# Row-scale products of the output projection moved from GpSimd to VectorE, row copies to ScalarE

## The chip, the cores and the metric

One core of a Trainium2 chip runs the whole layer. The metric is device microseconds (us) of one execution; less is better. A core has five engines that run side by side, each through its own list of instructions in order: PE (TensorE, matrix products), DVE (VectorE), ACT (ScalarE), POOL (GpSimd) and SP (SyncE, which here only starts transfers). They wait for each other through semaphores. Matrix results land in PSUM, everything else is held in SBUF, and weights come from HBM by DMA.

## The reference

The layer has an attention part (two head groups), an output projection with a residual, a norm with a router, and a mixture of 32 experts; then a final norm. The change lies where the output projection meets the second norm:

```python
mix = jnp.concatenate([o_a, o_b.astype(x.dtype)], axis=-1) @ w_out[l]     # 256 x 2048 @ 2048 x 2048
x = x + g1 * mix
h2 = rmsnorm(x, norm2_g[l]) * (1.0 + sc2) + sh2                             # sh2, sc2, g1: rows of 2048
x = x + g2 * hierarchical_moe(h2, w_router_group[l], b_router_group[l], w_router_expert[l], ...)
...
def rmsnorm(x, g):
    r = lax.rsqrt(jnp.mean(x32 * x32, axis=-1, keepdims=True) + EPS)
    return (x32 * r).astype(x.dtype) * g
```

The router takes h2 @ w_router (36 columns), picks one of 4 groups and 2 of 8 experts for each of the 256 tokens. Every expert's weights (w1, w3: 2048 x 512, w2: 512 x 2048, float32) are read once.

## The kernel before, in words

**Up to the output projection** (about 590 us) the kernel computes the modulation rows, the input projection and the head groups. The rows g1, norm2_g * (1 + sc2) and others lie in the tile `MOD`, each as four pieces of 512 on partitions 0, 32, 64, 96.

**The output projection** goes through four column blocks n = 0..3 of 512 columns. For each, `proj` adds up the products of all 2048 rows in two PSUM tiles `acc[t]` (t: the two halves of 128 tokens). A float32 product is made of three faster ones: the weight piece `wr` (two rows of tiles, 512 KB, L366) is rounded by ACT to `wH` (L376), DVE takes the remainder `wL` (L382), and PE multiplies wH with both parts of the left side and wL with one. One piece is 12 matmuls on PE (8 with wH, 4 with wL, L421; L407 in the last pieces of block 3), here called a step. `wr` has five buffers, wH and wL three each, so the conversions run up to three steps ahead of PE, and SP loads a new `wr` once DVE is done with an old one.

**Behind each block** `mix_out(n, ...)` is fed in pieces between the matmuls of the next block:
- POOL spreads a piece of `MOD` over all 128 partitions, `g1b` for g1 and `G2b` for the norm's row (L1010, two buffers each).
- For each t: DVE multiplies acc with g1b to `tmp` (L1021) and adds it to the residual `X` (L1022); ACT squares and sums a row (L1023, into `sp`); the row is multiplied by G2b to `xg` (the row-scale product: L1027 on POOL for n < 3, L1030 on DVE for n = 3); and `xg` is copied in another order of columns to `h2p`, the experts' input (the row copy: L1028 on ACT for n < 3, L1031 on POOL for n = 3).
- PE transposes xg to `ptr` in two pieces k2 (L1039), ACT copies each to `xt` (L1044; DVE does the very last one, L1042), and PE multiplies it with the router's weights, `pre` (L1049).

Beside block 1 stand two small products of the router's constant row, `pc` (L1062, L1065, con L1067).

**After block 3** the sums in `sp` become the norm's factor (`rsq`: L184, L185, a power, on POOL), DVE picks the experts in a chain of some 50 small instructions, and PE starts on the experts: `gather` (L1248), up (L1272), down (L1366). The experts' weights come through eight SBUF tiles of 2 MB, `r2t` (four; loads start during the projection) and `r3t` (four; in space that the projection's tiles leave), and three tiles `r4t` of 1 MB.

**Order.** The front and the experts are written out by hand on PE and SP. In the stretch of the output projection a scheduler orders every engine's list by its own estimates when the kernel is built, so a moved instruction also moves others. On POOL, the broadcast and the ordinary arithmetic belong to two pieces of code: the builder puts an instruction `ISA` without operands ahead of the first of the other kind.

Of the kernel before, what the change touches and what calls it, by code (L numbers as in the profile page):

```python
# [7 lines left out]
F32 = mybir.dt.float32  # L8
# [3 lines left out]
AF = mybir.ActivationFunctionType  # L12
OP = mybir.AluOpType
# [3 lines left out]
P = 128  # L17
# [93 lines left out]
def block_kernel(ctx: ExitStack, tc: tile.TileContext, x, w_mod, w_gate, w_in, w_ab, w_out, w_router, w1, w3, w2, w2_last,  # L111
                 vecs, rows, small, consts, out, dbg=None):
    nc = tc.nc
# [325 lines left out]
    def proj(form, lh=None, ll=None, before=None, end=False):  # L439
        acc = acc_pair(ps_acc, "acc")  # L440
        for q in range(4):
            step(acc, form, lh or hHb, ll or hLb, 0, NJ - 1, before, end and q == 3)
            ada_n()
        if form == "T":
            return acc
        drain_urgent()
        return acc
# [548 lines left out]
    wp = lst.enter_context(tc.tile_pool(name="wp", bufs=1, side="right", reuse_waits="tile"))  # L996
# [12 lines left out]
    def bcast(dst, src, n):  # L1009
        nc.gpsimd.partition_broadcast(dst, src[32 * n:32 * n + 1])  # L1010
        return dst

    sp = wp.tile([P, 2, 4], F32, name="sp")
    pre = ps_w.tile([P, 2, 36], F32, name="pre", tag="pre")

    def mix_out(n, acc, g1b, G2b):
        xg = [wq.tile([P, 512], F32, name="xg", tag="xg", bufs=2) for _ in range(2)]
        for t in range(2):
            xs = X2[:, t, n * 512:(n + 1) * 512]
            tmp = wq.tile([P, 512], F32, name="tmp", tag="tmp", bufs=2)  # L1020
            nc.vector.tensor_tensor(tmp, acc[t], g1b, op=OP.mult)  # L1021
            nc.vector.tensor_tensor(xs, xs, tmp, op=OP.add)  # L1022
            nc.scalar.activation(tmp, xs, AF.Square, accum_out=sp[:, t, n:n + 1])  # L1023
            hd = h2p[:, t, :, 32 * n:32 * n + 32].rearrange("p j q -> p q j")
            xv = xg[t].rearrange("p (q j) -> p q j", j=NJ)
            if n < 3:
                nc.gpsimd.tensor_tensor(xg[t], xs, G2b, op=OP.mult)  # L1027
                nc.scalar.activation(hd, xv, AF.Copy)  # L1028
            else:
                nc.vector.tensor_tensor(xg[t], xs, G2b, op=OP.mult)  # L1030
                nc.gpsimd.tensor_copy(hd, xv)  # L1031
        for _ in range(OY):
            yield 1
        for k2 in range(2):
            pt = ps_w.tile([P, 2, T], F32, name="ptr", tag="w", bufs=2)
            for t in range(2):
                for a in range(2):
                    k = 2 * k2 + a
                    nc.tensor.transpose(pt[:, a, t * P:(t + 1) * P], xg[t][:, k * P:(k + 1) * P], ident)  # L1039
            xt = wq.tile([P, 2, T], F32, name="xt", tag="xt", bufs=2)  # L1040
            if n == 3 and k2:
                nc.vector.tensor_copy(xt, pt)  # L1042
            else:
                nc.scalar.activation(xt, pt, AF.Copy)  # L1044
            yield 1
            for a in range(2):
                m = 4 * n + 2 * k2 + a
                for t in range(2):
                    nc.tensor.matmul(pre[:, t], xt[:, a, t * P:(t + 1) * P], WR[:, m], start=m == 0 and t == 0,  # L1049
                                     stop=m == NJ - 1, skip_group_check=True)  # L1050
            yield 1

    for n in range(4):
        g1b = bcast(wq.tile([P, 512], F32, name="g1b", tag="g1b", bufs=2), MOD[:, 0], n)
        G2b = bcast(wq.tile([P, 512], F32, name="G2b", tag="G2b", bufs=2), MOD[:, 1], n)
        if n:
            acc = proj("B", mixH, mixL, end=n == 3)
        urgent.append(mix_out(n, acc, g1b, G2b))
        if n == 1:
            pc = ps_w.tile([P, 2, 64], F32, name="pc", tag="w", bufs=2)  # L1060
            for j in range(NJ):
                nc.tensor.matmul(pc[0:1, 0, 0:36], S2[:, j:j + 1], WP[:, j], start=j == 0, stop=j == NJ - 1)  # L1062
            cr = wp.tile([1, 36], F32, name="cr")
            nc.scalar.activation(cr, pc[0:1, 0, 0:36], AF.Copy)
            nc.tensor.matmul(pc[:, 1, 0:36], ones[0:1], cr, start=True, stop=True)  # L1065
            con = wp.tile([P, 36], F32, name="con")
            nc.vector.tensor_tensor(con, pc[:, 1, 0:36], SM[:, S_RG:S_RG + 36], op=OP.add)  # L1067
# [339 lines left out]
    for t in range(2):  # L1407
        for n in range(4):
            xs = X2[:, t, n * 512:(n + 1) * 512]
# [63 lines left out]
```

## Time and profile before

| what | us |
|---|---|
| three timed runs | 1648.83, 1653.0, 1654.01 (median 1653.0) |
| profiled execution, its own time | 1649.8 |
| its span, from the first to the last instruction of the program | 1648.1 |
| PE busy | 1509.4 (92%) |
| DVE busy | 695.3 (42%) |
| ACT busy | 369.3 (22%) |
| POOL busy | 115.5 (7%) |
| HBM read | 584.73 MB, 356 GB/s over the span |

A start time in a row counts from the first instruction of the program. Busy time says how long an engine was at work, not whether anybody waited for it; PE busy counts matmuls that overlap and runs of half clock alike. What the engines waited for stands in brackets behind a row of the timeline: [idle time before it <- who ended it]. "issue" there means that no other engine is seen to have held it. PEclk is the granted share of PE's full clock of 2.4 GHz: 1.00 is that, 0.50 is 1.2 GHz.

### The profile page before, as it was taken

To read this page: it belongs to the slowest core of one execution; us is meant where nothing else is said; L and a number is where in the kernel's file an instruction comes from. 1 tells how busy PE (TensorE), PEld (TensorE's weight loads), DVE (VectorE), ACT (ScalarE), POOL (GpSimd) and SP (SyncE) were. 2 spreads that over 40 slices of the span, in tenths; PEclk is the share of its full clock that TensorE was granted. 3 is DMA by queue.
4 is the path that set the end of the run, shared out by engine and by line. 5 is a ranking of instruction groups with operands and counts; after the bars stand their busy time and mean duration, and the time that the engine had idled before them with its cause. 6 is when DMAs were issued, how large, how long until landed. Compare 5 with 4: busy or idle time off the path is not lost. (4 is left out here: it accounts for less than half of the span.)

```text
span 1648.1 us, 20660 instructions
## 1 busy us (share of the span) xinstructions
PE 1509.4 (92%) x8517; PEld 892.8 (54%) x8517; DVE 695.3 (42%) x1085; ACT 369.3 (22%) x745; POOL 115.5 (7%) x139
## 2 busy tenths in 40 slices
PE   3999989799789979799999999999999999899996
PEld 1788857688678867644443444444344344244432
DVE  4677797777555653513222313322231231232223
ACT  3444453363333544200100000010000000000002
POOL 1000033232111011100000000000000000000002
PEclk9999999899899998899999999999999999899998
DMA  9989688587677565579999999999999999999995
GB/s 353 371 335 369 250 325 318 209 328 286 262 302 271 204 232 212 237 301 376 415 427 429 426 428 427 429 426 428 428 427 427 427 428 427 427 426 427 426 420 217
DMA packets 74359, 588.50 MB, mean 357 GB/s; under 512 B 14084, under 2 KB 14468, under 8 KB 36372
## 3 DMA queue, kind: packets, MB, share of 16 engines
q1 hardware_dynamic: 68596, 581.88, 86.7%
q10 hardware_dynamic: 5664, 5.24, 1.0%
q8 instruction: 69, 1.13, 0.3%
q14 instruction: 30, 0.25, 0.0%
HBM read 584.73 MB, written 2.10 MB: 356 GB/s over the span
## 5 line engine op out<-in xcount | busy, mean ns | idle before, releaser
L1272 PE MATMUL h<-r2t,heT 128*64 128x512 f32 x1024 | 333.6, 600 | 9.9 <-issue 6.2
L1272 PE MATMUL h<-r3t,heT 128*64 128x512 f32 x1024 | 330.4, 594 | 1.1 <-DMA r3t<-in_w_dram 1.1
L382 DVE TENSOR_TENSOR wL<-wr,wH 128x1024 fp32r<-128x1024 f32 x144 | 178.2, 1242 | 110.1 <-ACT wH L376 84.5
L1272 PEld LDWEIGHTS h<-r2t,heT 128*64 128x64 f32 x1024 | 105.1, 138 | 157.3 <-issue 150.9
L376 ACT ACTIVATE wH<-wr 128x1024 fp32r<-128x1024 f32 x144 | 151.9, 1057 | 150.1 <-PE acc L421 70.7
L1272 PEld LDWEIGHTS h<-r3t,heT 128*64 128x64 f32 x1024 | 104.4, 137 | 147.0 <-issue 143.6
L1366 PE MATMUL po<-r2t,hidT 128*64 128x512 f32 x488 | 157.7, 594 | 3.7 <-ACT hidT L1289 3.7
L1366 PE MATMUL po<-r3t,hidT 128*64 128x512 f32 x448 | 147.2, 594 | 3.7 <-ACT hidT L1289 3.7
L1248 PEld LDWEIGHTS pgt<-ohr,h2p 128*128 128x128 f32 x1024 | 117.4, 194 | 16.6 <-issue 16.6
L1248 PE MATMUL pgt<-ohr,h2p 128*128 128x128 f32 x1024 | 121.0, 280 | 2.0 <-DVE ohr L1229 2.0
L1304 DVE TENSOR_TENSOR po<-po,g2b 128x512 f32<-128x512 f32 x64 | 44.5, 695 | 182.7 <-PE po L1366 171.8
L1313 DVE TENSOR_TENSOR X<-X,py 128x512 f32<-128x512 f32 x128 | 82.2, 684 | 85.3 <-PE py L1311 85.3
L417 PE MATMUL acc<-hH,wH 128*128 128x256 f32 x640 | 101.1, 299 | 8.4 <-ACT wH L376 8.4
L417 PE MATMUL acc<-hH,wL 128*128 128x256 f32 x640 | 97.4, 293 | 9.9 <-DVE wL L382 9.9
L1280 DVE SCALAR_TENSOR_TENSOR eth<-eth,h 128x512 f32<-128x512 f32 x16 | 11.0, 688 | 221.4 <-ACT eth L1279 221.4
L1279 ACT ACTIVATE eth<-h 128x512 f32<-128x512 f32 x16 | 9.6, 597 | 407.5 <-PE h L1272 407.5
L417 PEld LDWEIGHTS acc<-hH,wH 128*128 128x128 f32 x640 | 86.5, 198 | 24.6 <-ACT wH L376 12.5
L417 PE MATMUL acc<-hL,wH 128*128 128x256 f32 x640 | 97.0, 293 | 0.0
L417 PEld LDWEIGHTS acc<-hH,wL 128*128 128x128 f32 x640 | 85.3, 195 | 20.2 <-DVE wL L382 12.1
L417 PEld LDWEIGHTS acc<-hL,wH 128*128 128x128 f32 x640 | 86.1, 197 | 5.5 <-issue 5.0
L1366 PEld LDWEIGHTS po<-r2t,hidT 128*64 128x64 f32 x488 | 49.1, 137 | 69.9 <-issue 64.5
L1305 ACT ACTIVATE ob<-po 128x512 fp32r<-128x512 f32 x64 | 38.2, 597 | 213.2 <-DVE po L1304 213.2
(354 smaller groups left out, 1724.8 us busy)
## 6 DMA issues: line engine op xcount, KB each, us to landing
r2t<-in_w_dram SPq DMA_DIRECT2D x90, 2048.0 KB
r3t<-in_w_dram SPq DMA_DIRECT2D x88, 2048.0 KB
at<-in_w_gate_dram SPq DMA_DIRECT2D x64, 1024.0 KB
wr<-in_w_in_dram SPq DMA_DIRECT2D x112, 512.0 KB
mt<-in_w_mod_dram SPq DMA_DIRECT2D x32, 1024.0 KB
wr<-in_w_out_dram SPq DMA_DIRECT2D x32, 512.0 KB
r2t<-in_w_dram SPq DMA_DIRECT2D x9, 1024.0 KB
r3t<-in_w_dram SPq DMA_DIRECT2D x8, 1024.0 KB
```

Of the source, the lines that this page charges most:

```text
L376: nc.scalar.activation(H, rw, AF.Copy)
L382: nc.vector.tensor_tensor(Lf[:, :cut], rf_[:, :cut], Hf[:, :cut], op=OP.subtract)
L417: nc.tensor.matmul(acc[b], wt[:, j - j0, b * P:(b + 1) * P], ht, start=st and b % 2 == 0, stop=sp_, skip_group_check=True)
L1248: nc.tensor.matmul(pg_[:, jj], h2p[:, t, 4 * j4 + jj], ohr[:, t], start=t == 0, stop=t == 1)
L1272: nc.tensor.matmul(hx[64 * i:64 * i + 64], heT[:, j, 64 * i:64 * i + 64], wt[i][:, jj], start=j == 0, stop=j == NJ - 1, tile_position=(0, ...
L1279: nc.scalar.activation(th, h1, AF.Tanh, scale=0.5)
L1280: nc.vector.scalar_tensor_tensor(th, th, 1.0, h1, op0=OP.add, op1=OP.mult)
L1304: nc.vector.tensor_tensor(po, po, g2b[n], op=OP.mult)
L1305: nc.scalar.activation(ob[0][:, s], po, AF.Copy)
L1313: nc.vector.tensor_tensor(xs, xs, py, op=OP.add)
L1366: nc.tensor.matmul(po[n][64 * i:64 * i + 64], hT[:, c, 64 * i:64 * i + 64], wt[c, i][:, n * 512:(n + 1) * 512], start=c == 0, stop=c == 3, ...
```

## The change

The row-scale product xg is now made by DVE in all four blocks, right behind the residual's sum. The row copy to h2p is made by ACT in all four: for n < 3 at its old place in the text, for n = 3 from a list `late`, behind the copy of the second transposed piece. POOL keeps the broadcasts. Behind the last broadcast (n = 3) it makes a product of 128 x 2 numbers into a tile `warm` that nobody reads; it belongs to the ordinary arithmetic, as the norm's two instructions do.

```diff
+    late = []
+
     def mix_out(n, acc, g1b, G2b):
...
             xv = xg[t].rearrange("p (q j) -> p q j", j=NJ)
+            nc.vector.tensor_tensor(xg[t], xs, G2b, op=OP.mult)
             if n < 3:
-                nc.gpsimd.tensor_tensor(xg[t], xs, G2b, op=OP.mult)
                 nc.scalar.activation(hd, xv, AF.Copy)
             else:
-                nc.vector.tensor_tensor(xg[t], xs, G2b, op=OP.mult)
-                nc.gpsimd.tensor_copy(hd, xv)
+                late.append((hd, xv))
...
                 nc.scalar.activation(xt, pt, AF.Copy)
+            if k2:
+                for hd, xv in late:
+                    nc.scalar.activation(hd, xv, AF.Copy)
             yield 1
...
         G2b = bcast(wq.tile([P, 512], F32, name="G2b", tag="G2b", bufs=2), MOD[:, 1], n)
+        if n == 3:
+            nc.gpsimd.tensor_scalar(wp.tile([P, 2], F32, name="warm"), G2b[:, 0:2], 1.0, 0.0, op0=OP.mult, op1=OP.add)
```

Instructions outside of the projection stand as before on every engine, and SP's list is the same row for row. Line numbers of the changed kernel are up to 6 higher (L1039 is L1040, L1049 is L1053, L1010 is the same).

POOL through the blocks, from the broadcast of g1b for block 2 to that of G2b for block 3 (numbers tell the buffers apart; an `ISA` without operands changes the code):

```order
 L1010 ISA g1b_5881<-MOD_61 128x512
-L1027 ISA
-L1027 TENSOR_TENSOR xg_5689<-X2_5247,G2b_5671 128x512
-L1027 TENSOR_TENSOR xg_5690<-X2_5247,G2b_5671 128x512
-L1010 ISA
 L1010 ISA G2b_5883<-MOD_61 128x512
-L1027 ISA
-L1027 TENSOR_TENSOR xg_5897<-X2_5247,G2b_5675 128x512
-L1027 TENSOR_TENSOR xg_5898<-X2_5247,G2b_5675 128x512
-L1010 ISA
 L1010 ISA g1b_6067<-MOD_61 128x512
 L1010 ISA G2b_6069<-MOD_61 128x512
```

The products are gone and with them the changes of code between broadcasts; one such change is left, ahead of the product `warm` behind the last row.

PE while block 1 is multiplied, at the transposes and router products of block 0:

```order
+L421 MATMUL acc<-wH,mix 128x512 x4
+L1040 MATMUL ptr<-KC,xg 128x128 x8
+L421 MATMUL acc<-wH,mix 128x512 x4
+L421 MATMUL acc<-wL,mix 128x512 x2
+L1053 MATMUL pre<-WR,xt 128x36 x8
+L421 MATMUL acc<-wL,mix 128x512 x2
 L421 MATMUL acc<-wH,mix 128x512 x8
 L421 MATMUL acc<-wL,mix 128x512 x4
 L421 MATMUL acc<-wH,mix 128x512 x8
 L421 MATMUL acc<-wL,mix 128x512 x4
-L421 MATMUL acc<-wH,mix 128x512 x7
-L1039 MATMUL ptr<-KC,xg 128x128 x8
```

The eight transposes stand 27 matmuls earlier than before, in the step that comes two steps sooner; the router products follow in the same step.

ACT at the same place, before:

```order
L376 ACTIVATE wH<-wr 128x1024 x4
L1023 ACTIVATE tmp,sp<-X_5247 128x512 x2
L376 ACTIVATE wH<-wr 128x1024 x2
L1028 ACTIVATE h2p<-xg 128x32x16 x2
L1044 ACTIVATE xt<-ptr 128x512 x2
L376 ACTIVATE wH<-wr 128x1024 x2
```

and now:

```order
L376 ACTIVATE wH<-wr 128x1024 x4
L1025 ACTIVATE tmp,sp<-X_5247 128x512
L1030 ACTIVATE h2p<-xg 128x32x16
L1025 ACTIVATE tmp,sp<-X_5247 128x512
L1030 ACTIVATE h2p<-xg 128x32x16
L1045 ACTIVATE xt<-ptr 128x512 x2
L376 ACTIVATE wH<-wr 128x1024 x4
```

Two conversions of weights that stood ahead of the copies now stand behind them. DVE has the two products of block 0 between the sums X and five conversions wL; the order of the conversions among themselves is kept. In block 1, ACT's start of the transfer into `MOD` (L1068, which overwrites the row that POOL's last broadcast reads) moves ahead of the copies xt.

## Rows read from the trace of the kernel before

**Rows 1.** Busy time by stretch: us, busy of each engine, clock, DMA, GB/s.
```profile
core 0: us, PE busy (x) PEld busy (x) DVE busy (x) ACT busy (x) POOL busy (x), PEclk, DMA share, GB/s
619.50:629.50 10.00, 9.66 (x34) 8.34 (x35) 1.23 (x1) 3.99 (x5) 1.96 (x2) 0.50 0.00 0
663.00:684.00 21.00, 19.50 (x98) 16.12 (x97) 6.36 (x7) 7.08 (x10) 1.26 (x1) 1.00 0.26 97
684.00:705.00 21.00, 11.03 (x52) 9.81 (x50) 11.24 (x50) 2.65 (x8) 3.46 (x4) 0.59 1.00 426
730.00:1640.00 910.00, 863.61 (x4366) 379.60 (x4362) 240.41 (x378) 72.87 (x159) 14.01 (x16) 0.99 0.98 416
```

**Rows 2.** Timeline of PE, 595 to 740 us: start, duration, engine, line, names, [idle].
```profile
602.52 1.98 PE L421 MATMUL acc<-wH,mix 128*128 128x512 f32 x8
...
605.24 1.98 PE L421 MATMUL acc<-wH,mix 128*128 128x512 f32 x8
...
619.48 0.90 PE L1039 MATMUL ptr<-KC,xg 128*128 128x128 f32 x3 [9.77 <-POOL xg L1027]
...
627.39 2.98 PE L421 MATMUL acc<-wH,mix 128*128 128x512 f32 x8
...
631.22 1.20 PE L1062 MATMUL pc<-WP,S 128*1 128x36 f32 x32
...
641.87 1.03 PE L1039 MATMUL ptr<-KC,xg 128*128 128x128 f32 x8
...
644.01 1.98 PE L1049 MATMUL pre<-WR,xt 128*128 128x36 f32 x16 [0.40 <-ACT xt L1044]
...
665.28 0.44 PE L1039 MATMUL ptr<-KC,xg 128*128 128x128 f32 x2 [1.50 <-POOL xg L1027]
...
686.10 0.63 PE L1039 MATMUL ptr<-KC,xg 128*128 128x128 f32 x4 [1.51 <-DVE xg L1030]
687.92 1.12 PE L1039 MATMUL ptr<-KC,xg 128*128 128x128 f32 x4 [1.20 <-DVE xg L1030]
689.36 3.63 PE L1049 MATMUL pre<-WR,xt 128*128 128x36 f32 x16 [0.32 <-ACT xt L1044]
```

**Rows 3.** Timeline of POOL, 560 to 1000 us.
```profile
604.57 1.21 POOL L1010 PARTITION_BROADCAST g1b<-MOD  x1
618.17 2.49 POOL L1027 TENSOR_TENSOR xg<-X,G2b 128x512 f32<-128x512 f32 x2 [12.39 <-issue]
626.56 0.80 POOL L1010 PARTITION_BROADCAST G2b<-MOD  x1 [5.90 <-issue]
...
689.36 0.74 POOL L185 TENSOR_TENSOR r<-r,nhalf 128x2 f32<-128x2 f32 x1
```

**Rows 4.** Timeline of DVE, from 595 us and, apart, from 604.2 to 606.5 us.
```profile
605.04 1.68 DVE L382 TENSOR_TENSOR wL<-wr,wH 128x1024 fp32r<-128x1024 f32 x1
...
641.62 1.23 DVE L382 TENSOR_TENSOR wL<-wr,wH 128x1024 fp32r<-128x1024 f32 x1 [1.49 <-ACT wH L376]
...
685.27 0.68 DVE L1030 TENSOR_TENSOR xg<-X,G2b 128x512 f32<-128x512 f32 x1
```

**Rows 5.** Timeline of ACT, from 595 us.
```profile
604.08 0.63 ACT L1023 ACTIVATE tmp<-X 128x512 f32<-128x512 f32 x1 [1.21 <-DVE X L1022]
604.62 0.19 ACT L1023 ACTIVATION_READ_ACCUMULATOR tmp<-X 128x1 f32 x1
...
619.46 2.33 ACT L1028 ACTIVATE h2p<-xg 128x512 f32<-128x512 f32 x2 [11.14 <-POOL xg L1027]
621.59 1.09 ACT L1044 ACTIVATE xt<-ptr 128x512 f32<-128x512 f32 x2
```

**Rows 6.** Timeline of SP, 585 to 700 us.
```profile
677.90 7.32 SPq L1266 DMA_DIRECT2D r3t<-in_w_dram  x4
```

**Rows 7.** SP's queue, 660 to 1640 us: us waited, times, longest.
```profile
SPq L1266 <- PE po L1366: 313.6, 30, 16.3
SPq L1360 <- PE h L1272: 270.7, 29, 21.2
SPq L1266 <- DVE wL L382: 13.4, 1, 13.4
```

## The prediction

> **What bounds the kernel now.** I read the busy time by stretches first. From 730 to 1640 us the 16 DMA engines are 98% busy and PE runs at full clock: the experts' weights set the pace, and SP's queue waits there almost only for PE to give a tile back [rows 1, 7]. A change ahead of this stretch pays only if PE reaches the experts sooner and the loads move with it. So I looked at the stretch of the output projection, and there the loads are not the limit: from 663 to 684 us the DMA is 26% busy [rows 1]. The first r3t transfer, at 677.90, starts when DVE finishes the last wL of the projection (SP's 13.4 us wait) [rows 6, 7]. Loads follow PE there, not the other way.
>
> The timeline of PE shows what it waits for. Ahead of block 0's transposes it stands idle for 9.77 us, released by POOL's xg; in block 1 it waits 0.40 us, on ACT; in block 2 1.50, again on POOL; behind block 3 1.51 and 1.20, on DVE [rows 2]. After the long wait the granted clock is 0.50, that is 1.2 GHz, until 629.5 us, and the matmuls are stretched [rows 1]. POOL's own timeline says why xg is late: its last broadcast ends at 605.78, its first product starts at 618.17, 12.39 us later, with no engine holding it ("issue"), and between the two stands only the change of code; the change back costs 5.90 us ahead of the broadcast at 626.56 [rows 3].
>
> **What the change takes away and adds.** Off POOL go six products and two copies, and of the five changes of code between the first broadcasts and the norm one is left, ahead of `warm`. DVE gets six products of 0.68 us [rows 4], ACT two row copies of about 1.1 us (half of 2.33, rounded down for the overlap) [rows 5].
>
> *Block 0, replayed from the rows.* PE starts the step that now holds the transposes at 602.52; a step is 605.24 - 602.52 = 2.72 us, 0.227 per matmul [rows 2].
> - DVE: the sums X end at 605.12, and xg takes the place of the conversion at 605.04. That conversion took 1.68 us where one by itself takes 1.23 [rows 4]: 0.45 more, beside POOL's broadcast, which runs until 605.78 [rows 3]. I charge the same to the first product: xg for t = 0 is there at 605.04 + 0.68 + 0.45 = 606.2, for t = 1 at 606.8.
> - PE: four matmuls, until 603.4; wait for xg until 606.25; the transposes (1.03 us for eight [rows 2]; the second half may start at 606.85) end at 607.4; four and two matmuls, until 608.75.
> - ACT: square of t = 0 done by 604.8, row copy 606.2 to 607.3, square of t = 1 (0.63 and 0.19 to read the sum) to 608.1, row copy to 609.1, the two xt (1.09 together) at 609.7 and 610.2 [rows 5].
> - PE: waits for xt until 609.75, 1.0 us; 16 router products 1.98 us, until 611.7; two matmuls 0.45; then the two whole steps, the step of 627.39 and no slow clock: 612.2 + 3 x 2.72 = 620.35.
>
> Before, PE reached the same place (`pc`) at 631.22. Gain: 631.22 - 620.35 = 10.9 us. It is the 9.77 us of waiting and nearly 5 us of slow clock, less the two new waits of 2.8 and 1.0 us.
>
> The weights for these steps: wL for the two steps behind comes 1.75 us later on DVE, at about 608 and 609.2, needed by PE from 612 + 1.8 on. The next wH stands behind xt on ACT; if it takes as long as a row copy, it is ready at about 611.3, and needed at 617.6. The cover is 6 us; beyond it each us of delay costs one.
>
> *Block 1.* ACT still makes row copies ahead of xt, so the 0.40 us stays: 0, between -0.4 and +0.5. ACT's start of the transfer into MOD now stands ahead of xt, and waits until POOL's last broadcast is through. That broadcast is released by block 1's second product, which must also precede the row copy that stands just ahead on ACT; a broadcast takes 0.80 us [rows 3], the row copy 1.1. So it is hidden; without that cover xt and PE behind it wait up to 0.8 us.
>
> *Block 2.* The 1.50 us on POOL's xg go, but xt then waits for two squares, two row copies and a conversion on ACT. Bounds: 0 and 1.5 of gain; I take 0.5, nearer to block 1, where ACT is what is waited for.
>
> *Behind block 3.* ACT puts a row copy between the squares: 1.1 us each, of which all but some 0.2 fall into the waits for X; xt, and with it PE, is 0.2 us later (bounds: 1.1 late, 0.5 early, since DVE's second product no longer runs beside POOL's copies). The norm's power ended at 690.1 while PE was at `pre` until 693.0 [rows 2, 3]; it may come earlier and gain nothing. It needs no change of code, since `warm` made it long before. Cost: -0.2.
>
> *The clock.* Two waits, 2.8 and 1.0 us, are what PE still has in block 0. Behind block 3 waits of 1.51 and 1.20 us were enough for the clock to fall: the stretch from 684 to 705 was granted 0.59 on average [rows 1, 2]. If it falls in block 0, the slow matmuls first eat the 1.0 us in which PE would wait for xt. I take 0.2 us off; the upper bound is below.
>
> *The experts.* Everything up to the first expert is released by PE or DVE, so the start of the weight stream moves with them, one us for one.
>
> Sum: 10.9 + 0 + 0.5 - 0.2 - 0.2 = 11.0 us off the profiled execution's 1649.8, which makes 1638.8. That execution lies 3.2 us below the median of the three runs; off the median 1653.0 it is 1642.0, and that is the forecast. The range for this case alone is 1638 to 1646.
>
> **Two rules of the Trainium skill.** The sharing of ports: the rows show 0.45 us of delay for a DVE subtraction beside a broadcast [rows 4]. The page "SBUF — State Buffer", "Who interferes with whom", says that a VectorE instruction with two inputs in SBUF and a GpSimd instruction that reads SBUF lock each other out for a whole instruction. That speaks against the change, since the new products have two such inputs and broadcasts are what POOL keeps. By it the first product would start at 605.78, and the gain would be 0.3 us smaller; by the row it is as above. The delay in the trace agrees with a lock that was partly over.
>
> **Rivals.**
> 1. *The clock stays low in block 0.* After the new waits PE runs at 1.2 GHz for as long as it did from 619.5 to 629.5 [rows 1]. Ten us of matmuls at half clock cost 5 us: gain 6.0, 1647.0. For it: the waits behind block 3. Against: the waits in block 2 (1.50 us) were followed by a clock of 1.00 [rows 1, 2].
> 2. *The change of code is usually shorter than in this execution.* The other change that nothing else covers took 5.90 us [rows 3]. If block 0's normally takes that, the wait removed is 12.39 - 5.90 = 6.5 us shorter: gain 4.5, 1648.5. The page "GPSIMD Engine Reference", "Instruction dispatch", gives about 6 us for the first call of freshly loaded code, and would make this the normal case; the 12.39 us of the trace disagrees, the 5.90 agrees. Against: this execution was one of the fast ones.
> 3. *Hidden by the weight stream.* PE arrives 11 us sooner and waits for weights instead: 1653.0. For it: 98% busy DMA from 730 us on. Against: the idle DMA before, and SP's waits for PE.
> 4. *Slower.* PE now depends in each block on DVE's product and on ACT's row copies, which stand ahead of xt. If it waits in blocks 0 to 2 as I compute for block 0 (3.8 us), and the clock then falls for 10 us each time (5 us), that is 3 x 8.8 = 26.4 us, against 9.77 + 0.40 + 1.50 + 5 = 16.7 now: 9.7 us slower, 1662.7. It decides when two of the three blocks do so (17.6). For it: the low clock behind block 3 after DVE's products. Against: in blocks 1 and 2 ACT's copies stood ahead of xt already, and PE waited 0.40 us for them.
>
> **Numbers.** My case 0.74, rival 1 0.08, rival 2 0.07, rival 3 0.06, rival 4 0.05. A difference under 0.3%, 5 us here, can't be told from none: below 1648 is faster, above 1658 slower. Faster: my case but for a small tail, and rival 1: 0.81; same: rivals 2 and 3 and that tail, 0.14; slower: 0.05. The range 1637 to 1649.5 takes in the first three cases and leaves out rivals 3 and 4 and the edges.
>
> **What would show it.** Right: POOL's broadcasts of all blocks without a gap of 6 us or more between them that nobody ends; PE's wait ahead of block 0's transposes near 2.8 us and ended by DVE's xg, then one near 1 us ended by ACT's xt; `pc` some 11 us earlier, and the first r3t transfer at about 667; the same 11 us still there at the end. Wrong: a granted clock of 0.50 over more than 5 us of block 0 (rival 1), r3t earlier but the end not (rival 3), waits of several us ahead of the transposes or router products of blocks 1 and 2 (rival 4), or conversions wL that PE waits for. A change of code ahead of the norm would be paid beyond its 2.9 us of slack (690.1 to 693.0).

## The result, and the profile after

| | median, us | lowest to highest | runs |
|---|---|---|---|
| before | 1650.92 | 1648.83 to 1654.01 | 4 |
| after | 1638.62 | 1637.43 to 1639.56 | 4 |

The ratio is 0.9946 (95%: 0.9921 to 0.997), taken over runs on the same chip; it is 9 us less, the medians of the table lie 12.3 apart. The forecast of 1642.0 lies 3.4 us above the median of after. The profiled execution of after took 1638.36 us, its span is 1636.7. The main rows follow, those of PE first (start, duration, line, names, [idle <- who ended it]); they answer to [rows 2].

```profile
603.96 1.94 PE L1040 MATMUL ptr<-KC,xg 128*128 128x128 f32 x8 [2.73 <-DVE xg L1028]
...
607.75 1.87 PE L1053 MATMUL pre<-WR,xt 128*128 128x36 f32 x16
...
618.29 1.20 PE L1068 MATMUL pc<-WP,S 128*1 128x36 f32 x32
...
627.29 1.08 PE L1053 MATMUL pre<-WR,xt 128*128 128x36 f32 x8 [1.13 <-ACT xt L1045]
...
653.88 1.08 PE L1053 MATMUL pre<-WR,xt 128*128 128x36 f32 x8 [0.49 <-ACT xt L1045]
...
673.02 0.63 PE L1040 MATMUL ptr<-KC,xg 128*128 128x128 f32 x4 [1.51 <-DVE xg L1028]
674.25 0.66 PE L1040 MATMUL ptr<-KC,xg 128*128 128x128 f32 x4 [0.61 <-DVE xg L1028]
675.97 3.63 PE L1053 MATMUL pre<-WR,xt 128*128 128x36 f32 x16 [1.06 <-ACT xt L1045]
```

The reader is to see that the 9.77 us ahead of block 0's transposes have become 2.73, ended by DVE; that a new 1.13 us stands in block 1, ended by ACT; that block 2's wait fell from 1.50 to 0.49; and that behind block 3 three small waits stand where three stood. POOL's timeline answers to [rows 3]:

```profile
604.58 1.63 POOL L1010 PARTITION_BROADCAST G2b<-MOD  x1 [1.17 <-DVE xg L1028]
622.60 1.23 POOL L1010 PARTITION_BROADCAST g1b<-MOD  x1 [16.38 <-DVE tmp L1023]
624.40 1.64 POOL L1010 PARTITION_BROADCAST G2b<-MOD  x1 [0.57 <-DVE xg L1028]
634.37 0.18 POOL L1061 TENSOR_SCALAR warm<-G2b 128x2 f32<-128x2 f32 x1 [8.34 <-issue]
674.80 0.19 POOL L184 TENSOR_SCALAR r<-r 128x2 f32<-128x2 f32 x1 [40.25 <-DVE r L1083]
```

No broadcast is late by a change of code any more; the one left, 8.34 us ahead of `warm`, is waited for by nobody. The busy time by stretch (us, busy of each engine, clock, DMA share, GB/s) answers to [rows 1]:

```profile
603.70:607.10 3.40, 3.14 (x12) 2.87 (x13) 3.40 (x4) 3.25 (x6) 1.63 (x1) 0.50 1.07 458
652.00:673.00 21.00, 19.01 (x94) 15.36 (x93) 7.69 (x10) 6.42 (x10) 0.00 (x0) 1.00 0.35 138
675.40:695.90 20.50, 12.85 (x51) 10.11 (x53) 7.52 (x43) 1.45 (x7) 0.42 (x1) 0.50 0.89 372
719.00:1629.00 910.00, 862.69 (x4364) 380.99 (x4360) 240.84 (x379) 73.28 (x160) 14.04 (x16) 1.00 0.98 416
```

and SP's timeline to [rows 6]:

```profile
664.82 7.06 SPq L1272 DMA_DIRECT2D r3t<-in_w_dram  x4
```

The clock is low for 3.4 us in block 0. The experts' stretch is the same to the digit, 98% and 416 GB/s, and the first r3t transfer leaves 13.1 us earlier.

Where the 11.4 us between the two spans came from is read by cutting both at the same instructions. The stretches, in us: up to the last matmul `psof` ahead of the projection's end (no instruction of it is changed); from there to DVE's row MOD (L1007, the row that G2b is spread from); to `pc` in block 1; to the first gather `pgt`; to the first product with r3t; to the end. The last column leaves out the part up to psof.

| kernel | to psof | to MOD | to pc | to pgt | to r3t | to the end | from psof |
|---|---|---|---|---|---|---|---|
| before | 591.1 | 9.3 | 30.8 | 69.9 | 25.4 | 921.6 | 1057.0 |
| after | 588.8 | 9.3 | 20.2 | 69.5 | 27.3 | 921.7 | 1047.9 |
| again | 589.8 | 9.2 | 20.4 | 69.4 | 27.4 | 922.0 | 1048.4 |
| blk0_pool | 590.5 | 9.3 | 31.8 | 68.6 | 25.1 | 921.7 | 1056.6 |
| load_only | 591.8 | 9.4 | 25.3 | 69.0 | 25.5 | 922.1 | 1051.4 |
| no_warm | 586.0 | 9.3 | 20.1 | 69.4 | 27.2 | 921.3 | 1047.3 |
| mod_later | 588.7 | 9.3 | 20.3 | 68.3 | 27.9 | 922.2 | 1048.0 |
| rw_alone | 589.0 | 5.7 | 20.7 | 69.4 | 25.5 | 922.4 | 1043.7 |
| all4 | 588.4 | 5.9 | 20.0 | 68.5 | 27.7 | 922.0 | 1044.1 |
| quiet | 589.8 | 5.2 | 25.4 | 69.1 | 27.3 | 921.7 | 1048.7 |
| late_pre | 586.4 | 5.3 | 20.8 | 69.4 | 27.3 | 921.6 | 1044.4 |
| best | 586.4 | 4.4 | 23.2 | 67.7 | 25.5 | 921.8 | 1042.6 |

So the change is worth 9.1 us in this pair of profiles: 10.6 in block 0, about 0.4 in the blocks behind, less 1.9 at the first experts. The other 2.3 us of the spans lie ahead of it, where the programs are alike: that part varies from 586.0 to 591.8 over all the kernels.

### The profile page after: what moved, and what is told of

The parts are those of the page before. It is cut to its first block, busy times and chain, and to the rows that moved or that the text cites. A ratio compares the mean times of both kernels' runs of the same rounds, so it can differ in the third digit from the quotient of the medians.

```text
span 1636.7 us, 20650 instructions
## 1 busy us (share of the span) xinstructions
PE 1506.1 (92%) x8517; PEld 889.3 (54%) x8517; DVE 697.3 (43%) x1091; ACT 371.2 (23%) x747; POOL 107.2 (7%) x132
## 3 DMA queue, kind: packets, MB, share of 16 engines
q8 instruction: 69, 1.13, 0.3%
## 5 line engine op out<-in xcount | busy, mean ns | idle before, releaser
L417 PEld LDWEIGHTS acc<-hH,wH 128*128 128x128 f32 x640 | 85.7, 196 | 25.5 <-ACT wH L376 12.8
L1372 PEld LDWEIGHTS po<-r2t,hidT 128*64 128x64 f32 x488 | 49.0, 137 | 69.9 <-issue 64.5
```

Of the source, the lines that this page charges most:

```text
L417: nc.tensor.matmul(acc[b], wt[:, j - j0, b * P:(b + 1) * P], ht, start=st and b % 2 == 0, stop=sp_, skip_group_check=True)
L1372: nc.tensor.matmul(po[n][64 * i:64 * i + 64], hT[:, c, 64 * i:64 * i + 64], wt[c, i][:, n * 512:(n + 1) * 512], start=c == 0, stop=c == 3, ...
```

## The experiments

All are edits of the kernel after, except where said; ratios are to the kernel before, with 95% intervals.

**again.** No edit, for the size and a second profile.

> The changed kernel once more, timed in five rounds. Between the two profiles 2.35 us of the 11.4 us had been gained before PE came to block 0's transposes, where the two programs are the same, and 1.8 us were lost at the first expert, where the clock stayed low in one of them for longer. If both are chance, the gain is what block 0 shows, less nothing: 10.6 us from block 0, 0.15 from blocks 1 and 2, 0.3 behind block 3, in all 11, a ratio of 0.9933. If the loss at the first expert belongs to the change, 9.3 us, 0.9944. If the front's 2.35 us belong to it, 13 us, 0.992.

Measured: 1638.69 us, ratio 0.9933 (0.9907 to 0.9959). The table's row repeats that of after within 0.5 us in every stretch behind psof, the longer 27.4 at the first experts included. That the loss came twice speaks for the second of the three cases, though 0.9933 is the first one's figure; the interval takes in all three.

**blk0_pool.** Block 0's two products go back to GpSimd, the rest stays:

```diff
-            nc.vector.tensor_tensor(xg[t], xs, G2b, op=OP.mult)
+            (nc.vector if n else nc.gpsimd).tensor_tensor(xg[t], xs, G2b, op=OP.mult)
```

> The changed kernel with block 0's two row-scale products back on GpSimd, blocks 1 to 3 as changed. Theory (block 0's one change of code is the whole gain): PE waits about 10 us ahead of block 0's transposes again, with a slow clock behind it, and the gain falls to 0.5 us, a ratio of 0.9997 (0.998 to 1.002). Rival (each of the changes of code and each GpSimd product costs its share): two of three blocks are still better, and 5 to 7 us of gain are left, 0.996.

Measured: 1646.74 us, 0.999 (0.9973 to 1.0007): no gain is left. The rows of POOL and PE:

```profile
617.32 2.49 POOL L1028 TENSOR_TENSOR xg<-X,G2b 128x512 f32<-128x512 f32 x2 [12.16 <-issue]
625.60 0.80 POOL L1010 PARTITION_BROADCAST G2b<-MOD  x1 [5.79 <-issue]
```

```profile
618.63 0.90 PE L1040 MATMUL ptr<-KC,xg 128*128 128x128 f32 x3 [9.50 <-POOL xg L1028]
```

They are [rows 2, 3] over again, 12.16 for 12.39 and 9.50 for 9.77. The rest of the change (blocks 1 and 2, block 3's row copies, `warm`) brings nothing that the times show.

**load_only.** DVE keeps all products, but block 0's must wait for a tiny product on GpSimd, and so for a change of code:

```diff
+        if n == 0:
+            nc.gpsimd.tensor_scalar(G2b[:, 0:2], G2b[:, 0:2], 1.0, 0.0, op0=OP.mult, op1=OP.add)
```

> The changed kernel, all products on VectorE, but behind block 0's broadcast GpSimd multiplies two columns of G2b by one in place, so that VectorE's product must wait for a change of code and a product of 128 x 2 numbers. Theory (it is the change of code that held PE, not the engine that multiplies): VectorE's product comes 8 to 12 us later, PE waits for it 6 to 10 us, and the gain goes: ratio 0.998 to 1.003. Rival (the slower products on GpSimd and their sharing of ports with VectorE were the cost): a product of two columns is 0.2 us, so at most 1 us is lost against the changed kernel, ratio 0.994.

Measured: 1643.35 us, 0.9973 (0.9956 to 0.999). DVE's and PE's rows:

```profile
616.45 1.29 DVE L1028 TENSOR_TENSOR xg<-X,G2b 128x512 f32<-128x512 f32 x2 [7.59 <-POOL G2b L1061]
```

```profile
617.29 1.09 PE L1040 MATMUL ptr<-KC,xg 128*128 128x128 f32 x4 [7.73 <-DVE xg L1028]
```

The wait came back (7.73 us) though DVE makes the product, so it is the change of code that PE waits for, not GpSimd's own 1.25 us for a product. But the ratio lies just below the expected 0.998 to 1.003, and only 5.0 of the 11.6 us between after and blk0_pool are lost up to `pc` (25.3 against 20.2 and 31.8). Transposes start 16.1 us behind the row MOD, in blk0_pool 18.8; 2.2 of these 2.7 us are there because POOL changes its code two broadcasts earlier (3.15 us behind the start of MOD's row instead of 5.36). And the clock is low for 6.8 us in block 0 instead of 17.1, which at half speed is worth up to 5.1. Why the clock came back sooner these runs do not tell.

**no_warm.** Without the tiny product:

```diff
-        if n == 3:
-            nc.gpsimd.tensor_scalar(wp.tile([P, 2], F32, name="warm"), G2b[:, 0:2], 1.0, 0.0, op0=OP.mult, op1=OP.add)
```

> The changed kernel without the tiny product, so that the change of code falls to the norm's first instruction. In the changed kernel the norm's factor was ready at 675.8 and first used at 679.7. Theory: the change takes 6 to 8.5 us from the sum at 674.7 on, the factor comes at 681.7 to 684.2, and everything behind it 2 to 4.5 us later: ratio to before 0.995 to 0.997. Rival 1 (with weights streaming at full rate it takes as long as the 12.4 us of block 0 before): 8 us later, 0.9985. Rival 2 (slack hides it): no difference from the changed kernel, 0.9935.

Measured: 1638.48 us, 0.9944 (0.9925 to 0.9964): nothing is lost, the expectation failed. POOL's timeline:

```profile
621.50 1.64 POOL L1010 PARTITION_BROADCAST G2b<-MOD  x1 [0.57 <-DVE xg L1028]
671.97 0.19 POOL L184 TENSOR_SCALAR r<-r 128x2 f32<-128x2 f32 x1 [48.83 <-DVE r L1081]
```

The norm's product starts when DVE's r is there, with no "issue" behind it. The instruction that changes the code, and the wait for r (L184: number of instructions in the whole program, ns of one, first and last start in us):

```profile
L184 POOLq MODIFY_POOL_CONFIG  x4: 11/69/127, 3.0 to 623.1; - x4
L184 POOLq EVENT_SEMAPHORE  x1: 17/17/17, 671.8 to 671.8; - x1
```

The change was started at 623.1, at the end of the last broadcast, and went by within the 48.83 us in which POOL waited for r: it does not stand behind the wait of the instruction that needs it. So `warm` hides a cost that was hidden anyway.

**mod_later.** ACT's start of the transfer into MOD goes to SP, much later:

```diff
-    nc.scalar.dma_start(MOD[0:P:32, 1], rows[:, 5])
...
+        if pr == 1:
+            nc.sync.dma_start(MOD[0:P:32, 1], rows[:, 5])
```

> The changed kernel, with the transfer into MOD that ScalarE started ahead of block 1's xt moved to the second pair of experts, on SP. In the changed kernel block 1 takes 0.84 us longer than before, PE waits 1.13 us for xt instead of 0.40, and xt stands behind that transfer, which starts when GpSimd's last broadcast ends, 0.5 us after the row copy. Theory (the transfer's wait is the cost): xt 0.5 us earlier and PE's wait down to 0.4 to 0.6 us, a gain of 0.6 us over the changed kernel. Rival (a conversion of 1.06 us that the scheduler now puts ahead of xt takes the same place): the wait stays near 1 us, no gain. Either way less than a time can show; PE's wait in block 1 decides.

Measured: 1637.94 us, 0.994 (0.992 to 0.996). By time it cannot be told from after; in PE's timeline block 1's wait is down to 0.25:

```profile
626.92 1.08 PE L1053 MATMUL pre<-WR,xt 128*128 128x36 f32 x8 [0.25 <-ACT xt L1045]
```

From `pc` to `pgt` it takes 68.3 us instead of 69.5. The first experts then take 27.9, with a clock that is low until 9.4 us beyond the first gather, so from psof nothing is gained (1048.0 and 1047.9).

**rw_alone.** RW is the row that DVE waits for ahead of block 0 (4 us, on a transfer, in before and after alike). The router's weights, asked for ahead of it on ACT's queue (in after WP at 582.62, WR at 589.63, RW at 590.01), go to SP's:

```diff
-    nc.scalar.dma_start(WR, w_router[:, 0])
...
-    nc.scalar.dma_start(WP, w_router[:, 1])
+    nc.sync.dma_start(WP, w_router[:, 1])
+    nc.sync.dma_start(WR, w_router[:, 0])
```

> The changed kernel, with the two transfers of router weights that stood ahead of RW in ScalarE's queue given to SP, so that RW comes alone. In the changed kernel VectorE stands about 4 us waiting for RW (L1007), and everything of block 0 is behind that: sums, products, transposes. Theory (block 0's new 2.7 us of PE waiting for xg is that wait handed on): RW lands 3 to 4 us sooner, PE's wait for xg goes to 0 to 0.5 us and with it the short stretch of slow clock; 3 to 4 us off the changed kernel, ratio to before 0.991. Rival (VectorE's chain of seven instructions is as long as the wait): PE still waits 2 us or more, 0.993.

Measured: 1635.43 us, 0.9923 (0.9895 to 0.9951). DVE's row of after, then DVE's and PE's rows of rw_alone:

```profile
602.67 1.75 DVE L1028 TENSOR_TENSOR xg<-X,G2b 128x512 f32<-128x512 f32 x2
```

```profile
594.66 0.69 DVE L1007 SCALAR_TENSOR_TENSOR MOD<-MOD,RW 128x512 f32<-128x512 f32 x1 [3.94 <-DMA RW<-in_rows_dram]
...
600.87 1.28 DVE L1028 TENSOR_TENSOR xg<-X,G2b 128x512 f32<-128x512 f32 x2
```

```profile
601.70 1.17 PE L1040 MATMUL ptr<-KC,xg 128*128 128x128 f32 x8 [0.21 <-DVE xg L1028]
```

The row MOD is there 5.7 us behind psof instead of 9.3, and PE's wait for xg falls from 2.73 to 0.21. What PE still waits for in block 0 of after is a transfer of 8 KB. From psof to the end it takes 4.2 us less than after: 3.1 of them up to `pc`, 1.8 at the first experts, and 0.7 are lost behind.

**all4.** mod_later and rw_alone together, the row copies last in the text, and the copies xt ahead of ACT's other work:

```diff
-            if n < 3:
-                nc.scalar.activation(hd, xv, AF.Copy)
-            else:
-                late.append((hd, xv))
+            late.append((hd, xv))
...
-                nc.scalar.activation(xt, pt, AF.Copy)
...
+                with tc.high_priority(XP):
+                    nc.scalar.activation(xt, pt, AF.Copy)
...
```

> The two edits together, with the row copies taken behind the router products in the program's text and xt given a higher priority, so that in block 0 one xt no longer stands behind both row copies. Theory: the two gains add, and block 0's 1.0 us between transposes and router products goes down too: 4 to 5 us off the changed kernel, ratio to before 0.990. Rival (what PE saves it loses at the first expert, where the start of the clock's return decides): 0.993.

Measured: 1634.41 us, 0.9916 (0.9887 to 0.9946); 1044.1 from psof. Both waits are down, block 0's to 0.51 and block 1's to 0.26, and the first experts take 27.7 instead of rw_alone's 25.5, so by the profile it is no better than rw_alone: the gains do not add, for the rival's reason.

**quiet.** Block 0's products stay on GpSimd, as in blk0_pool, and the first r2t (2 MB each) is sent for only once block 1's columns are written:

```diff
+                if (pr, q, m) == (0, 0, 0):
+                    nc.vector.tensor_copy(wt[1][:, 0, 0:1], X2[:, 0, 512:513])
```

> The kernel with block 0's products back on GpSimd, but the experts' prefetched tiles (r2t) loaded only after block 1, so that fewer weights move while GpSimd changes its code. So far the change took 5.7 to 6.0 us where the DMA moved 0 to 89 GB/s, 8.3 to 8.9 us at 205 to 216 GB/s, 11.9 to 12.4 us at 304 to 349 GB/s. Theory (the code comes through the same DMA engines, behind the weights): with half of the traffic 7 to 9 us instead of 12.2, and PE's wait ahead of block 0's transposes 4 to 7 us instead of 9.5. Rival (the long change belongs to the place in the program, not to the traffic): 12 us again. Its time is not compared, since the prefetch comes later.

Measured: 1632.48 us (1630.26 to 1640.16), 0.9907 (0.9874 to 0.994), by time as fast as the kernels with the products on VectorE. POOL's and PE's rows:

```profile
606.92 3.48 POOL L1028 TENSOR_TENSOR xg<-X,G2b 128x512 f32<-128x512 f32 x2 [6.89 <-issue]
616.39 0.80 POOL L1010 PARTITION_BROADCAST G2b<-MOD  x1 [5.99 <-issue]
```

```profile
610.45 0.77 PE L1040 MATMUL ptr<-KC,xg 128*128 128x128 f32 x5 [1.66 <-POOL xg L1028]
```

The change of code ahead of block 0's product takes 6.89 us instead of 12.16, and PE waits 1.66 instead of 9.50. Two things shorten the way: the row MOD, and so RW, is there 4.1 us sooner (3.6 in rw_alone), and the stretch to `pc` is 6.4 us shorter. The profiled execution was the slowest of the five (1640.16); what made the others 5 to 10 us faster was not traced.

**late_pre.** The kernel after with quiet's edit alone, to tell what it brings without a change of code that PE waits for.

> The kernel after (all four blocks' products on VectorE), with the one edit of quiet: the first experts' weights r2t are sent for only once block 1's columns are written. It tells what of quiet's time came from a shorter change of code. Theory A (holding the weights back gains only because GpSimd's change of code no longer queues behind them; here the only changes of code left wait for nobody): the ratio stays at that of the kernel after, 0.991 to 0.996. Rival B (holding them back gains by itself, since wr, r3t or the mix pass get the DMA engines): ratio 0.986 to 0.990, and the stretch from the first tmp to pc or the first expert is over 2 us shorter. Rival C (it costs: r2t lands late and the first expert waits): the first po over 1 us later, ratio over 0.996. The change of code in block 2 (8.3 us at 205 GB/s in the kernel after) is the same or shorter, and nobody waits for it.

Measured: 1634.83 us, 0.992 (0.9897 to 0.9943). The ratio is in theory A's range, but its reason is only half of it: by the profile 3.5 us are gained from psof on, all of it in the stretch to the row MOD (5.3 for 9.3). It is B's kind of gain, with RW in the place of wr.

**best.** rw_alone, mod_later and the held back r2t in one kernel.

> The kernel after with three edits at once: WP and WR asked for by SyncE so that RW lands without them on ScalarE's queue, the MOD transfer of the next stage moved off ScalarE's queue to SyncE in the second expert pair, and r2t sent for only after block 1. Theory: PE's waits ahead of block 0's transposes fall from 2.73 to under 0.6 us and block 1's from 1.13 to under 0.4, so block 0 and 1 are some 2 to 3 us shorter than in the kernel after by the profile, and the ratio is 0.989 to 0.993. Rival: the clock gives it back at the first expert pair (low for one step of 3.4 us more), ratio 0.993 as the kernel after.

Measured: 1633.21 us, 0.9915 (0.9893 to 0.9936), the shortest way from psof (1042.6). By time its interval overlaps that of after. Block 1's wait is 0.26 us, but block 0 has a slow stretch of the clock again (603.6 to 607.0, `pc` 2.4 us later than in late_pre), so its parts do not add up.

**What the length of a change of code goes with.** Three kernels' busy times over such stretches (the last number is what the DMA engines moved, in GB/s), of before, load_only and quiet:

```profile
605.78:618.17 12.39, 3.93 (x18) 2.92 (x16) 4.35 (x4) 2.11 (x4) 0.00 (x1) 0.77 0.78 302
620.66:626.56 5.90, 5.84 (x24) 5.47 (x25) 0.00 (x0) 2.93 (x4) 0.00 (x2) 0.50 0.00 0
```

```profile
604.36:616.23 11.87, 5.20 (x23) 3.96 (x22) 4.50 (x5) 3.36 (x6) 0.01 (x1) 0.90 0.86 348
```

```profile
600.03:606.90 6.87, 6.87 (x32) 5.69 (x31) 3.99 (x4) 4.33 (x7) 0.00 (x0) 1.00 0.59 177
610.40:616.39 5.99, 5.83 (x27) 5.16 (x28) 0.00 (x0) 2.96 (x4) 0.00 (x1) 0.65 0.23 81
```

The time between the end of POOL's instruction before and the start of the next is 5.9 us with nothing moved, 6.0 at 81 GB/s, 6.9 at 177, 11.9 at 348 and 12.4 at 302. (PE is idle in the long ones because it waits for them.) The two short ones are changes back to the broadcast, the three others changes into arithmetic, so these rows mix traffic with direction. Among the changes into arithmetic alone, the one ahead of `warm` takes 8.3 to 9.7 us at 190 to 234 GB/s in ten profiles, between those. quiet moved the traffic away at the same place of the program, and the time of the same change fell from 12.16 to 6.89. Whether the 2 MB transfers just ahead or the rate make it long is not separated, and how long a change into arithmetic takes with nothing moved no run shows.

## Why the prediction was right, and where it was not

**Block 0, the term that carries the sum: right.** Forecast 10.9, measured 10.6 (after) and 10.4 (again). PE's wait for DVE's xg was to be 2.8 us and is 2.73. The second wait, 1.0 us for xt, did not come: PE reached the router products at 607.75 with no idle time. The clock fell for 3.4 us instead, and the slow matmuls took the place of that wait, as the prediction had allowed; the block came out 0.3 us short, where 0.2 had been set for it. blk0_pool shows that this block is the whole gain, load_only that a change of code alone brings PE's wait back.

**Its price, read as fixed: it goes with the traffic.** The 12.39 us was taken from one execution, with rival 2 against it. Block 0's is long in every profile with r2t asked for just ahead (12.39, 12.16, 11.87), so rival 2 falls. The rival's figure, 5.90, is no shorter case of it: it is a change the other way, with nothing on the DMA engines. The page "GPSIMD Engine Reference" of the Trainium skill, "Instruction dispatch", gives about 6 us. The traces agree where little is moved (5.8 to 6.0 us at 0 to 88 GB/s, all changes back to the broadcast), and disagree above 300 GB/s (11.9 to 12.4).

**Block 1: the step failed that called the transfer into MOD hidden.** The prediction took POOL's last broadcast as 0.80 us, shorter than ACT's row copy of 1.1. ACT's timeline, and DVE's row at the same time:

```profile
624.39 1.12 ACT L1030 ACTIVATE h2p<-xg 128x512 f32<-128x512 f32 x1
626.07 0.53 ACTq L1074 DMA_DIRECT2D MOD<-in_rows_dram  x1
626.64 0.60 ACT L1045 ACTIVATE xt<-ptr 128x512 f32<-128x512 f32 x1 [1.13 <-PE acc L421]
```

```profile
624.15 1.22 DVE L382 TENSOR_TENSOR wL<-wr,wH 128x1024 fp32r<-128x1024 f32 x1
```

The broadcast took 1.64 us (624.40 to 626.04, the row of POOL above), because DVE's conversion had begun at 624.15 (see the shared port below); the 0.80 us was the row of a broadcast with DVE idle, and 1.21 stood in [rows 3] beside it. The transfer started at 626.07, and xt behind it; PE waited 1.13 us instead of 0.40. mod_later, which takes that start away, brings it to 0.25, so the cause is shown. The profile names "PE acc" as what ended ACT's wait: the transfer's start, which is no busy time, stands between. Block 1 took 0.8 us more; the bounds were -0.4 to +0.5, and "up to 0.8" without the cover.

**Block 2: the direction right, the size small.** 0.5 was taken, from 0 to 1.5; the stretch is 1.0 shorter and PE's wait is 0.49 instead of 1.50.

**Behind block 3: sign wrong by little.** 0.2 of loss was forecast, 0.3 of gain is measured. xt does wait longer, 1.06 for 0.32, but DVE's second product is less late, 0.61 for 1.20, as the bound for it said.

**`warm`: the reason was wrong.** "It needs no change of code, since `warm` made it long before" does not explain it: without `warm` it costs nothing either (no_warm). No number rested on it but the last sentence's warning of 2.9 us of slack, which was void.

**The experts: "one us for one" missed 1.9 us.** From pgt to the first r3t product, after takes 27.3 us and before 25.4. Its clock is low from 675.4 to 695.9, which is 8.1 us beyond the first gather (687.8). The stretch in before, and in rw_alone:

```profile
687.50:704.60 17.10, 9.42 (x41) 8.83 (x42) 7.72 (x44) 1.21 (x4) 1.99 (x3) 0.50 0.99 421
```

```profile
672.00:689.00 17.00, 9.03 (x41) 8.84 (x41) 7.67 (x43) 1.59 (x5) 0.80 (x2) 0.50 1.00 420
```

They last until 3.5 and 4.2 us beyond the first gather (701.1, 684.8), and these kernels take 25.4 and 25.5. So the 1.9 us go with when the clock comes back. All twelve profiles agree: where it is low until 2.8 to 4.2 us beyond the first gather, the stretch takes 25.1 to 25.5 us, where until 8.0 to 9.4, 27.2 to 27.9. It is not the products' place: rw_alone has them all on VectorE and 25.5, quiet has two on GpSimd and 27.3. Why it lasts longer in some kernels, after and again among them, stays open. From there to the end nothing is lost (921.6 and 921.7 us), so rival 3 falls; rivals 1 and 4 fall with 3.4 us of low clock and waits of 1.13 and 0.49.

**The total.** The terms 10.9 + 0 + 0.5 - 0.2 - 0.2 became 10.6 - 0.8 + 1.0 + 0.3 (the clock's term is part of block 0's), and the experts took 1.9 back: 9.1 us, but for rounding, where 11.0 were forecast. That the spans differ by 11.4, so near to the forecast, is luck: the part that the change does not touch was 2.3 us shorter in the profile of after, and that made up for the 1.9 that the forecast missed. Of the 3.4 us by which 1642.0 missed the median of after, 2.1 are that it was taken off 1653.0, where the median of before is 1650.92.

**The shared port.** The 0.45 us charged to the first product is seen: block 0's two took 1.75 us where two undisturbed ones take 1.28 (the rows of after and of rw_alone above), beside broadcasts. The page "SBUF — State Buffer" of the Trainium skill, "Who interferes with whom", calls the pair of ports that VectorE and GpSimd share an exclusive lock. The traces agree, in both directions. From 585 to 700 us the twelve profiles have 96 broadcasts. The 34 that began with no DVE instruction of two operands in SBUF (wL, X, xg) under way took 0.80 us; the other 62 ended 0.66 to 0.67 us behind the end of that instruction, however long that was. A DVE instruction of this kind that began while a broadcast ran was longer by what the broadcast still had to run, less 0.28 us (0.46 for 0.74, 0.36 for 0.63, nothing for 0.20); the 0.3 us by which the prediction set a full lock apart from its row is that 0.28. So what a broadcast takes hangs on what DVE is at when it starts; in block 1 that was a conversion.

## What to carry to other kernels

Where an engine stands idle and the profile names only "issue", look at what it must fetch before it can go on, and at who else is on the DMA engines then: here moving two small products away from a change of code gave the 9 us, and holding back a 2 MB prefetch shortened the same change to 6.9 us. The start of a transfer in ACT's list held up what stood behind it (1.13 us of PE's time, 0.25 without it), and its cover must be taken from the slowest row of the instruction that it waits for, or from what DVE does at that instruction's start. After a wait is gone, ask what feeds the engine that is now waited for: block 0's last 2.7 us were an 8 KB row behind weights.

## What was not expected of the hardware

- GpSimd's change of code into arithmetic took 6.9 us with 177 GB/s on the DMA engines and 11.9 to 12.4 with 302 to 348; the change back took 5.8 to 6.0 at 0 to 88 GB/s.
- A change of code runs ahead of the wait of the instruction that needs it: hidden in 48.83 us of waiting in no_warm.
- The same broadcast of a row took 0.80 to 1.74 us on POOL, by the DVE instruction under way at its start; in after the one that block 1's wait hangs on took 1.64.
